# Forgetting attention: gate and mask in one tile that VectorE adds, and the second score products of two long query tiles on 64 rows each

## The chip, the cores and the metric

The kernel runs on one core of a Trainium2 chip. The metric is device time in microseconds (us), the median over runs of the same program. A core has TensorE (matrix products: a weight load brings a stationary operand of up to 128 rows and 128 columns into the array, a matmul then streams the columns of the moving operand through it), VectorE (DVE in the profile), ScalarE (ACT), GpSimd (POOL) and SyncE (SP), which mostly issues DMA transfers. Matmul results go to PSUM, which has banks of 512 float32 columns on 128 partitions; everything else on the chip lies in SBUF, also with 128 partitions.

## The reference

A decoder trunk of two layers on 512 tokens of width 1024. Each layer is a half-step SwiGLU feed-forward, a mixer of three parallel groups (short convolution, HGRN2 recurrence, forgetting attention called FoX), one output projection over all groups, and a second feed-forward. The change is in FoX, which has 8 heads of 64:

```python
log_f = jax.nn.log_sigmoid((f_logit + f_bias).astype(f32))
cum = jnp.cumsum(log_f, axis=1).transpose(0, 2, 1)
def block(i):                                   # 128 queries
    ...
    s = (jnp.einsum('bhqd,bhkd->bhqk', qb, kh).astype(f32)
         + (cb[..., :, None] - cum[..., None, :]))
    s = jnp.where(qpos[:, None] >= kpos[None, :], s, MASK_VALUE)
    p = jax.nn.softmax(s, axis=-1)
    return jnp.einsum('bhqk,bhkd->bhqd', p.astype(vh.dtype), vh)
```

The term of the query, `cb`, is the same for all keys of a row, so softmax doesn't see it; the kernel adds only minus the running sum of each key.

## The kernel before

All large products are made in a format with a rounded high part and a low part ("fp32r"): an operand x is split into hi (the rounded copy) and lo (x − hi), and a product is the sum of three, hi·hi, hi·lo and lo·hi. Weights are streamed from HBM, split by ScalarE (the cast to hi) and VectorE (the subtraction for lo), and multiplied by TensorE (lines 499, 505, 506 in `mm3`, 603 in `stream_steps`).

In each layer's mixer the steps of attention are woven with dense products (the remaining input projections, the convolution, the first three quarters of the output projection) by generators: `BESIDE` says how many pieces of dense work stand between two steps of `fox_attend`. Matmuls of the attention and of the pieces beside it are put in one written order by `follow("p", ...)`. The other engines' queues are ordered by the scheduler.

Heads are worked off in order. `fox_prep` (lines 1926 to 1950) makes the operands of one head two heads ahead: four transposes bring queries and keys of the head (64 rows each) to the partitions, ScalarE writes hi, VectorE lo, and six DMAs on SP's queue (line 1949) spread their halves over the tiles QA = [hi of q; lo of q], KA = [hi of k; hi of k], QB = [hi of q; two rows of ones] and KB = [lo of k; two rows of the sums]. QA·KA is hi·hi + lo·hi, on 128 rows; QB·KB is hi·lo plus the gate, on 66 rows. The two rows are minus the running sums, hi and lo, from `fox_decay`; they come from DRAM by a small DMA (line 1934), and GpSimd writes the ones (line 1935).

A head has two steps p, each with two query tiles u of 128 queries; query tile i = 2p + u sees n = 128(i + 1) keys. `scores(h, p)` makes for each query tile the product with QA and then the one with QB, into one PSUM area (line 1974 in the profile is the helper that records them): p = 0 has 128 and 256 columns in one bank, p = 1 has 384 and 512 in a bank each. There are two banks for it ("sc"), which the steps share in turn. Then `maximum` (line 1983) lets VectorE add the mask (zeros, and −1e30 above the diagonal in the last 128 columns) and take the row maximum in one pass, in place in PSUM; ScalarE takes the exponential (line 377), which frees the bank, and the weights are normalised (lines 2000 to 2006). Two steps later `turn` transposes the weights (line 2015), splits them (2030, 2031), and `values` multiplies them with V (line 2040).

The order within one round is: turn of step k, half of the values of the head before, preparation of head h + 2, scores of step k + 2, the other half of the values. HGRN2, earlier in the same stage, has products on tiles of 64 rows and 64 columns (line 1723 and others), of which four lie side by side on the array.

Of the kernel before, what the change touches and what calls it, by code (L numbers as in the profile page):

```python
# [8 lines left out]
F32 = mybir.dt.float32  # L9
# [5 lines left out]
ALU = mybir.AluOpType  # L15
# [201 lines left out]
def halves(x):  # L217

    return x.rearrange("p (h t) -> p h t", h=2)
# [17 lines left out]
def inner(x):  # L237

    return x.rearrange("p (b t h) -> p b h t", h=2, t=CH)
# [12 lines left out]
class Trunk:  # L252
# [40 lines left out]
    def build_consts(self, scratch):  # L293

        nc = self.nc
        c = self.const

        self.ones_blk = c.tile([P, P], F32R, tag="ones_blk", name="ones_blk")
        nc.vector.memset(self.ones_blk.bitcast(F32), 0.0)
        for h in range(2):  # L300
            r = slice(64 * h, 64 * h + 64)
            nc.vector.memset(self.ones_blk[r, r].bitcast(F32), 1.0 / 64)

        self.heads2 = c.tile([P, 2], F32, tag="heads2", name="heads2")
        nc.vector.memset(self.heads2, 0.0)
        for h in range(2):
            nc.vector.memset(self.heads2[64 * h : 64 * h + 64, h : h + 1], 1.0)

        self.smask = c.tile([P, T], F32, tag="smask", name="smask")
        nc.vector.memset(self.smask, 1.0)  # L310
        nc.vector.memset(self.smask.rearrange("p (c t) -> p c t", t=CH)[:, :, 0:1], 0.0)
        self.ones_row = nc.const_aps.tensor(1.0, [NH, T], F32)
        self.mask = c.tile([P, T], F32, tag="mask", name="mask")
        nc.vector.memset(self.mask[:, : 3 * P], 0.0)

        self.lmask = c.tile([P, 6, CH], U8, tag="lmask", name="lmask")
# [24 lines left out]
        b = scratch(F32)[:, :CH]  # L341
        for l in range(1, 7):
            nc.vector.tensor_scalar(
                a, xf, scalar1=float(2 ** (l - 1)), scalar2=None, op0=ALU.is_ge
            )
            nc.vector.tensor_scalar(b, xf, scalar1=float(2**l), scalar2=None, op0=ALU.is_lt)
            nc.vector.tensor_mul(a, a, b)
            nc.vector.tensor_mul(self.lmask[:, l - 1, :], a, own)

        nc.vector.tensor_scalar(  # L350
            inner(self.mask[:, 3 * P :])[:, 0], halves(later), scalar1=-1e30, scalar2=None, op0=ALU.mult
        )

    def n(self, s):
        self.uid += 1
# [996 lines left out]
    def mix(self, l, w, w_out, conv_w, out_gain, q_gain, k_gain, f_bias, next_gain, logits):  # L1352
# [3 lines left out]
        with tc.tile_pool(name=self.n("mix"), bufs=1) as mp:  # L1356
# [48 lines left out]
            with tc.tile_pool(name=self.n("hg"), bufs=1) as hp:  # L1405
                self.tt, self.tb = "t", 10

                b, kb, q, S = (pair(mp, tag) for tag in ("b", "kb", "q", "S"))
                negc = mp.tile([NH, 2, T], F32R, tag="n", name=self.n("negc"))
                bz = features([(H_F, 256)], ("mm", "mm"), lambda: self.end_norm(self.bank("pt"), hp))  # L1410
                if l == 0:
                    self.lower_bounds(logits, hp.tile([P, T], F32, tag="t", name=self.n("lb"), bufs=10))
# [416 lines left out]
    def fox_decay(self, mp, hp, zf, negc):  # L1829
# [9 lines left out]
        for j in range(4):  # L1839
            nc.tensor.transpose(cb[:NH, j * P : (j + 1) * P], lf[:, j, :], self.ident)  # L1840
        c = hp.tile([P, T], F32, tag="t", name=self.n("fc"), bufs=self.tb)[:NH, :]
        nc.vector.tensor_tensor_scan(c, self.ones_row, cb[:NH, :], 0.0, op0=ALU.mult, op1=ALU.add)
        nc.scalar.activation(negc[:, 0, :], c, AF.Copy, scale=-1.0)
        nc.vector.scalar_tensor_tensor(
            out=negc[:, 1, :], in0=c, scalar=-1.0, in1=negc[:, 0, :], op0=ALU.mult, op1=ALU.subtract
        )
        self.negc = self.dram.tile([NH, 2, T], F32, tag="negc", name=self.n("negc"))
        nc.sync.dma_start(self.negc, negc.bitcast(F32))

    def fox_qkv(self, mp, hp, tokens, half):  # L1850

# [67 lines left out]
    def fox_prep(self, pool, h, qk, g):  # L1919
# [6 lines left out]
        tl = lambda tag: self.mp.tile([P, T], F32R, tag=tag, name=self.n(tag))  # L1926
        hi, lo = tl("b0"), tl("b1")
        if h % 2:
            QA, KA, QB, KB = (tl(t) for t in ("S0", "S1", "q0", "q1"))
        else:  # L1930
            A = self.mp.tile([P, 2, T], F32R, tag="n", name=self.n("A"))
            QA, KA, QB, KB = A[:, 0, :], A[:, 1, :], tl("kb0"), tl("kb1")
        QB, KB = QB[:66, :], KB[:66, :]
        nc.sync.dma_start(KB[64:66, :].bitcast(F32), self.negc[h])
        nc.gpsimd.memset(QB[64:66, :].bitcast(F32), 1.0)
        b = self.bank("pt")
        for i in range(4):
            self.follow("p", nc.tensor.transpose(
# [3 lines left out]
        nc.vector.scalar_tensor_tensor(  # L1942
            out=lo, in0=b, scalar=g, in1=hi, op0=ALU.mult, op1=ALU.subtract
        )
        for to, src in (
            (QA[:64], hi[:64]), (KA[:64], hi[64:]), (KA[64:], hi[64:]), (QB[:64], hi[:64]),
            (QA[64:], lo[:64]), (KB[:64], lo[64:]),
        ):
            nc.sync.dma_start(to.bitcast(F32), src.bitcast(F32))
        return QA, QB, KA, KB  # L1950

    def fox_attend(self, pool, half, g):

# [8 lines left out]
            ops[h] = self.fox_prep(pool, h, half[h // 4], g)  # L1962

        def scores(h, p):
            QA, QB, KA, KB = ops[h]
            pb = pool.tile([P, (384, 896)[p]], F32, tag=f"P{p}", name=self.n("P"), bufs=2)
            s2 = lambda tag: pool.tile([P, 2], F32, tag=tag, name=self.n(tag), bufs=2)
            nm, rs = s2("nm"), s2("rs")
# [6 lines left out]
            for u in range(2):  # L1975
                i = 2 * p + u
                c, n = slice(i * P, (i + 1) * P), (i + 1) * P
                mm(at[u], QA[:, c], turned_in(KA[:, :n]), start=p == 1 or u == 0, stop=False)
                mm(at[u], QB[:, c], turned_in(KB[:, :n]), start=False, stop=True)
            to = [pb[:, :P], pb[:, P:]] if p == 0 else [pb[:, : 3 * P], pb[:, 3 * P :]]  # L1980

            def maximum(u):
                m = nc.vector.tensor_tensor_reduce(
                    at[u], at[u], self.mask[:, (3 - 2 * p - u) * P :], scale=-1.0, scalar=1e30,
                    op0=ALU.add, op1=ALU.min, accum_out=nm[:, u : u + 1],
                )
                self.maxima = m.ins.name
# [13 lines left out]
            for u in range(2):  # L2001
# [3 lines left out]
                else:  # L2005
                    nc.vector.tensor_scalar(to[u], to[u], scalar1=rs[:, o], scalar2=None, op0=ALU.mult)
            weights[h, p] = to

        def turn(h, p):

# [63 lines left out]
                nc.vector.tensor_sub(self.yl[kt], fo, self.yh[kt])  # L2074

        steps = [(h, p) for h in range(NH) for p in range(2)]
        prep(0)
        yield
        scores(0, 0)
# [155 lines left out]
```

## Time and profile before

| | |
|---|---|
| median of 3 runs | 1731.06 us (1731.04 to 1732.46) |
| the profiled execution's own time | 1730.99 us |
| its span in the profile | 1729.2 us |
| TensorE, matmuls: busy | 1724.9 us |
| VectorE busy | 1420.3 us |
| ScalarE busy | 1009.4 us |
| GpSimd busy | 176.2 us |
| attention stages (two layers) | about 434 to 530 us and 1290 to 1387 us |

In the rows of the profile L1974 is line 1974 of the kernel; PE is a matmul, PEld a weight load, which overlaps matmuls. Rows of the timeline give start, length, engine, line, operation, output and inputs, shapes, and in square brackets the idle time before it with what ended it. Matmuls are pipelined, so their lengths overlap: the distance from start to start tells what one costs. Rows of the groups give the count, the busy time in all, the mean in ns, and the idle time before them.

### The profile page before, as it was taken

To read this page: it belongs to the slowest core of one execution; us is meant where nothing else is said; L and a number is where in the kernel's file an instruction comes from. 1 tells how busy PE (TensorE), PEld (TensorE's weight loads), DVE (VectorE), ACT (ScalarE), POOL (GpSimd) and SP (SyncE) were. 2 spreads that over 40 slices of the span, in tenths; PEclk is the share of its full clock that TensorE was granted. 3 is DMA by queue.
4 is the path that set the end of the run, shared out by engine and by line. 5 is a ranking of instruction groups with operands and counts; after the bars stand their busy time and mean duration, and the time that the engine had idled before them with its cause. 6 is when DMAs were issued, how large, how long until landed. Compare 5 with 4: busy or idle time off the path is not lost.

```text
span 1729.2 us, 32556 instructions
## 1 busy us (share of the span) xinstructions
PE 1724.9 (100%) x13161; PEld 1623.3 (94%) x13161; DVE 1420.3 (82%) x1988; ACT 1009.4 (58%) x1406; POOL 176.2 (10%) x174
## 2 busy tenths in 40 slices
PE   9999999999999999999999999999999999999999
PEld 8999999888888999999989999998988889999998
DVE  7988787678888898888689887876888889788884
ACT  5565565465776565566446655555667765655651
POOL 0011120100000112012001111201000000120210
PEclk9999999999999999999999999999999999999999
DMA  7778784243543967878266787933435447678672
GB/s 218 185 149 194 185 178 111 72 128 87 151 129 98 241 149 157 206 163 171 86 193 168 178 180 178 191 87 80 116 96 146 127 126 203 159 150 228 144 161 97
DMA packets 249766, 262.28 MB, mean 152 GB/s; under 512 B 25816, under 2 KB 221152, under 8 KB 249616
## 3 DMA queue, kind: packets, MB, share of 16 engines
q1 hardware_dynamic: 197344, 192.02, 37.2%
q0 software_dynamic: 52256, 68.19, 24.4%
q8 instruction: 103, 1.69, 0.4%
q14 instruction: 47, 0.39, 0.1%
q10 hardware_dynamic: 16, 0.00, 0.0%
HBM read 226.15 MB, written 2.17 MB: 132 GB/s over the span
## 4 chain that ended last, share of the span: by engine, by line
PE 100%; DMA 0%; DVE 0%; issue 0%
PE mm L499 11%; PE mm L505 11%; PE mm L506 11%; PE mm L603 9%; PE pt L499 7%; PE pt L506 7%; PE pt L505 7%; PE sc L499 6%; PE sc L506 6%; PE sc L505 6%; PE po L505 3%; PE po L499 3%; PE po L506 3%; PE po L603 2%; PE sc L1974 1%; PE po L2040 1%
## 5 line engine op out<-in xcount | busy, mean ns | idle before, releaser
L1075 DVE TENSOR_TENSOR hl<-w,hl 128x1024 fp32r<-128x1024 f32 x279 | 341.4, 1224 | 97.6 <-ACT hl L1071 95.8
L1071 ACT CAST hl<-w 128x1024 fp32r<-128x1024 f32 x279 | 292.8, 1049 | 205.5 <-PE mm L506 50.3
L486 DVE TENSOR_TENSOR hl<-st,hl 128x1024 fp32r<-128x1024 f32 (+3 forms) x151 | 159.1, 1056 | 95.9 <-ACT hl L480 95.2
L480 ACT CAST hl<-st 128x1024 fp32r<-128x1024 f32 (+3 forms) x151 | 137.4, 913 | 155.5 <-PE po L506 37.0
L499 PE MATMUL mm<-xc,hl 128*128 128x256 f32 x698 | 191.5, 275 | 0.0
L505 PE MATMUL mm<-xc,hl 128*128 128x256 f32 x696 | 191.5, 275 | 0.0
L506 PE MATMUL mm<-xc,hl 128*128 128x256 f32 x696 | 191.4, 275 | 0.0
L499 PE MATMUL pt<-xc,hl 128*128 128x256 f32 x546 | 150.1, 275 | 0.0
L505 PE MATMUL pt<-xc,hl 128*128 128x256 f32 x544 | 149.7, 275 | 0.0
L506 PE MATMUL pt<-xc,hl 128*128 128x256 f32 x544 | 149.6, 275 | 0.0
L499 PEld LDWEIGHTS mm<-xc,hl 128*128 128x128 f32 x698 | 133.9, 192 | 0.1
L505 PEld LDWEIGHTS mm<-xc,hl 128*128 128x128 f32 x696 | 133.6, 192 | 0.0
L506 PEld LDWEIGHTS mm<-xc,hl 128*128 128x128 f32 x696 | 133.6, 192 | 0.0
L499 PE MATMUL sc<-xc,hl 128*128 128x256 f32 (+1 forms) x466 | 127.9, 275 | 0.0
L505 PE MATMUL sc<-xc,hl 128*128 128x256 f32 x464 | 127.7, 275 | 0.0
L506 PE MATMUL sc<-xc,hl 128*128 128x256 f32 x464 | 127.6, 275 | 0.0
L603 PE MATMUL mm<-hl,x 128*128 128x512 f32 x432 | 107.2, 383 | 0.0
L499 PEld LDWEIGHTS pt<-xc,hl 128*128 128x128 f32 x546 | 104.6, 192 | 0.3
L505 PEld LDWEIGHTS pt<-xc,hl 128*128 128x128 f32 x544 | 104.4, 192 | 0.3
L506 PEld LDWEIGHTS pt<-xc,hl 128*128 128x128 f32 x544 | 104.4, 192 | 0.0
L499 PE MATMUL mm<-x,hl 128*128 128x512 f32 x272 | 103.4, 381 | 0.0
L506 PE MATMUL mm<-x,hl 128*128 128x512 f32 x272 | 103.1, 379 | 0.0
(540 smaller groups left out, 5310.9 us busy)
## 6 DMA issues: line engine op xcount, KB each, us to landing
w<-in_ffn_w_in_dram SPq DMA_DIRECT2D x124, 512.0 KB, 6.0
w<-in_ffn_w_out_dram POOLq DMA_DIRECT2D x50, 512.0 KB, 9.5
w<-in_ffn_w_out_dram SPq DMA_DIRECT2D x49, 512.0 KB, 4.4
st<-in_ffn_w_out_dram SPq DMA_DIRECT2D x39, 512.0 KB, 3.6
st<-in_w_mix_in_dram SPq DMA_DIRECT2D x72, 256.0 KB, 3.1
st<-in_ffn_w_in_dram SPq DMA_DIRECT2D x71, 256.0 KB, 3.2
w<-in_ffn_w_in_dram POOLq DMA_DIRECT2D x29, 512.0 KB, 10.0
w<-S POOLq DMA_DIRECT2D x29, 512.0 KB, 5.1
```

Of the source, the lines that this page charges most:

```text
L480: a = nc.scalar.copy(hi, src[:, c : c + w])
L486: b = nc.vector.tensor_sub(lo, src[:, c : c + w], hi)
L499: i = nc.tensor.matmul(acc[:, c], ah, bh[:, c.start // 2 : c.stop // 2, :], start=first and c.start == 0, stop=False, skip_group_check=True,)
L505: nc.tensor.matmul(acc, ah, bl, start=False, stop=False, skip_group_check=True)
L506: i = nc.tensor.matmul(acc, al, bh, start=False, stop=last, skip_group_check=True)
L603: self.follow("p", self.nc.tensor.matmul(acc, *((w, woven(x)) if toks is None else (x[:, toks], woven(w))), start=k == 0 and id(acc) not i ...
L1071: A(nc.scalar.copy(hi, src))
L1075: return lambda: V(nc.vector.tensor_sub(lo, src, hi))
L1974: mm = lambda *a, **k: E(nc.tensor.matmul(*a, skip_group_check=True, **k))
L2040: E(nc.tensor.matmul(self.ob[:, o * P : (o + len(at)) * P], half[2][:, j, h].rearrange("p a d -> p (a d)"), turned_in(part[:, at[0] : at[- ...
```

## The change

The gate leaves TensorE. The sums are written once, in float32, to DRAM. `fox_gate(h, p)` broadcasts the first n of them to all 128 partitions, for each of the two query tiles, by a DMA on GpSimd's queue, and writes −1e30 above the diagonal in the last 128 columns by a select on GpSimd. VectorE's pass adds this tile where it added the mask. The gates of head h + 1 are asked for right after the scores of head h for the same p, and go into the same tiles.

The second product then has hi of q and lo of k alone: 64 rows. KB becomes [lo of k; lo of k]. For p = 0 both products are on 128 rows (QA·KB is hi·lo + lo·lo). For p = 1 the first of the two query tiles takes rows 0 to 63, the second rows 64 to 127; for that, QA holds the last 128 queries with its halves swapped. The two first products of a step are now issued ahead of the two second ones. `fox_prep` has eight DMAs, three of them for the swapped queries and the second copy of lo, and no longer the small one and the memset.

```diff
-        self.mask = c.tile([P, T], F32, tag="mask", name="mask")
-        nc.vector.memset(self.mask[:, : 3 * P], 0.0)
...
-        nc.vector.tensor_scalar(
-            inner(self.mask[:, 3 * P :])[:, 0], halves(later), scalar1=-1e30, scalar2=None, op0=ALU.mult
-        )
...
-        nc.scalar.activation(negc[:, 0, :], c, AF.Copy, scale=-1.0)
-        nc.vector.scalar_tensor_tensor(
-            out=negc[:, 1, :], in0=c, scalar=-1.0, in1=negc[:, 0, :], op0=ALU.mult, op1=ALU.subtract
-        )
-        self.negc = self.dram.tile([NH, 2, T], F32, tag="negc", name=self.n("negc"))
-        nc.sync.dma_start(self.negc, negc.bitcast(F32))
+        nc.scalar.activation(inner(negc), turned_out(c), AF.Copy, scale=-1.0)
+        self.negc = self.dram.tile([NH, T], F32, tag="negc", name=self.n("negc"))
+        nc.sync.dma_start(self.negc, negc)
...
-            QA, KA, QB, KB = (tl(t) for t in ("S0", "S1", "q0", "q1"))
+            QA, KA, KB = (tl(t) for t in ("S0", "S1", "q1"))
         else:
             A = self.mp.tile([P, 2, T], F32R, tag="n", name=self.n("A"))
-            QA, KA, QB, KB = A[:, 0, :], A[:, 1, :], tl("kb0"), tl("kb1")
-        QB, KB = QB[:66, :], KB[:66, :]
-        nc.sync.dma_start(KB[64:66, :].bitcast(F32), self.negc[h])
-        nc.gpsimd.memset(QB[64:66, :].bitcast(F32), 1.0)
+            QA, KA, KB = A[:, 0, :], A[:, 1, :], tl("kb1")
...
+        n, last = slice(0, 3 * P), slice(3 * P, T)
         for to, src in (
-            (QA[:64], hi[:64]), (KA[:64], hi[64:]), (KA[64:], hi[64:]), (QB[:64], hi[:64]),
-            (QA[64:], lo[:64]), (KB[:64], lo[64:]),
+            (QA[:64, n], hi[:64, n]), (KA[:64], hi[64:]), (KA[64:], hi[64:]), (QA[64:, n], lo[:64, n]),
+            (KB[:64, n], lo[64:, n]), (QA[64:, last], hi[:64, last]), (QA[:64, last], lo[:64, last]),
+            (KB[64:], lo[64:]),
         ):
             nc.sync.dma_start(to.bitcast(F32), src.bitcast(F32))
...
+    def fox_gate(self, h, p):
+        nc = self.nc
+        wide = lambda pool, tag: pool.tile([P, T], F32, tag=tag, name=self.n("W"))
+        if p == 0:
+            w = wide(self.mp, "kb0")
+            to = [w[:, :P], w[:, P : 3 * P]]
+        else:
+            to = [wide(self.mp, "q0")[:, : 3 * P], wide(self.const, "mask")]
+        for u, w in enumerate(to):
+            n = (2 * p + u + 1) * P
+            nc.gpsimd.dma_start(w, self.negc[h : h + 1, :n].to_broadcast([P, n]))
+        for w in to:
+            d = w[:, w.shape[-1] - P :].rearrange("p (t h) -> p t h", h=2)
+            nc.gpsimd.affine_select(
+                d, d, pattern=[[-1, CH], [-CH, 2]], compare_op=ALU.is_ge, fill=-1e30,
+                base=0, channel_multiplier=1,
+            )
+        self.gates[p] = to
...
                 mm(at[u], QA[:, c], turned_in(KA[:, :n]), start=p == 1 or u == 0, stop=False)
-                mm(at[u], QB[:, c], turned_in(KB[:, :n]), start=False, stop=True)
+            for u in range(2):
+                i = 2 * p + u
+                c, n = slice(i * P, (i + 1) * P), (i + 1) * P
+                r = slice(0, P) if p == 0 else (slice(0, 64), slice(64, P))[u]
+                mm(at[u], QA[r, c], turned_in(KB[r, :n]), start=False, stop=True)
...
-                    at[u], at[u], self.mask[:, (3 - 2 * p - u) * P :], scale=-1.0, scalar=1e30,
+                    at[u], at[u], gate[u], scale=-1.0, scalar=1e30,
...
             weights[h, p] = to
+            if h + 1 < NH:
+                self.fox_gate(h + 1, p)
...
+        self.gates = {}
+        for p in range(2):
+            self.fox_gate(0, p)
         prep(0)
```

More of the change, by code (lines that the diff above doesn't have):

```diff
@@ L1408, in mix @@
                 b, kb, q, S = (pair(mp, tag) for tag in ("b", "kb", "q", "S"))
-                negc = mp.tile([NH, 2, T], F32R, tag="n", name=self.n("negc"))
+                negc = mp.tile([NH, T], F32, tag="n", name=self.n("negc"))
                 bz = features([(H_F, 256)], ("mm", "mm"), lambda: self.end_norm(self.bank("pt"), hp))
@@ L1944, in fox_prep @@
         )
+        n, last = slice(0, 3 * P), slice(3 * P, T)
         for to, src in (
-            (QA[:64], hi[:64]), (KA[:64], hi[64:]), (KA[64:], hi[64:]), (QB[:64], hi[:64]),
-            (QA[64:], lo[:64]), (KB[:64], lo[64:]),
+            (QA[:64, n], hi[:64, n]), (KA[:64], hi[64:]), (KA[64:], hi[64:]), (QA[64:, n], lo[:64, n]),
+            (KB[:64, n], lo[64:, n]), (QA[64:, last], hi[:64, last]), (QA[:64, last], lo[:64, last]),
+            (KB[64:], lo[64:]),
         ):
             nc.sync.dma_start(to.bitcast(F32), src.bitcast(F32))
-        return QA, QB, KA, KB
+        return QA, KA, KB
+    def fox_gate(self, h, p):
[16 more added lines that the diff above has]
+        self.gates[p] = to
     def fox_attend(self, pool, half, g):
@@ L1964, in scores @@
         def scores(h, p):
-            QA, QB, KA, KB = ops[h]
+            QA, KA, KB = ops[h]
+            gate = self.gates[p]
             pb = pool.tile([P, (384, 896)[p]], F32, tag=f"P{p}", name=self.n("P"), bufs=2)
```

## The prediction

> **What bounds the kernel now.** I read the page first, the busy line and the chain that ended last.
>
> ```profile
> span 1729.2 us, 32556 instructions
> PE 1724.9 (100%) x13161; PEld 1623.3 (94%) x13161; DVE 1420.3 (82%) x1988; ACT 1009.4 (58%) x1406; POOL 176.2 (10%) x174
> PE 100%; DMA 0%; DVE 0%; issue 0%
> ```
>
> TensorE is busy from end to end and the chain never leaves it: what its own stream gains or loses, the kernel gains or loses, until another engine makes it wait. Second, the attention stage of the first layer (the second is alike) by windows, with columns for busy time and count of each engine:
>
> ```profile
> 434.00:530.00 96.00, 96.00 (x532) 85.76 (x530) 82.31 (x192) 69.24 (x152) 3.11 (x6) 1.00 0.51 133
> ```
>
> VectorE is busy for 82 of 96 us and GpSimd for 3: TensorE bounds here too, with full clock, VectorE not far behind. Third, the timeline of one score step of two long query tiles (head 4, layer 1 of 2), matmuls and then weight loads. A is the first product, on 128 rows; the one that reads kb is the second, on 66; I call them A0, B0, A1, B1.
>
> ```profile
> 493.32 0.41 PE L1974 MATMUL sc<-A 128*128 128x384 f32 x1
> 493.56 0.33 PE L1974 MATMUL sc<-kb,kb 66*128 66x384 f32 x1
> 493.73 0.38 PE L1974 MATMUL sc<-A 128*128 128x512 f32 x1
> 493.95 0.38 PE L1974 MATMUL sc<-kb,kb 66*128 66x512 f32 x1
> 494.17 0.38 PE L603 MATMUL mm<-hy,hl 128*128 128x512 f32 x1
> ...
> 493.29 0.19 PEld L1974 LDWEIGHTS sc<-A 128*128 128x128 f32 x1
> 493.40 0.19 PEld L1974 LDWEIGHTS sc<-kb,kb 66*128 66x128 f32 x1
> 493.57 0.19 PEld L1974 LDWEIGHTS sc<-A 128*128 128x128 f32 x1
> 493.73 0.19 PEld L1974 LDWEIGHTS sc<-kb,kb 66*128 66x128 f32 x1
> 493.95 0.41 PEld L603 LDWEIGHTS mm<-hy,hl 128*128 128x128 f32 x2
> ```
>
> Busy times overlap, so I go by starts. A matmul of 512 columns holds the array 0.22 us (493.73 to 493.95), one of 384 0.17 (493.56 to 493.73). The next weight load starts as the running matmul starts (493.73 and 493.95 stand in both lists), so it is hidden. A0's record is 0.08 longer than its likes: it began to stream at 493.40, 0.11 after its load, which is what a bare load costs. The step takes 494.17 − 493.40 = 0.77 us. There are 16: 8 heads, 2 layers.
>
> **The change, part by part.** *The halves.* B0 and B1 move to 64 rows each and stand side by side. If they run together, the shorter is hidden: −0.16 us a step. But TensorE goes from whole-array products to half-array ones and back. What does such a switch cost? The kernel has other products on parts of the array; the timeline at one of them, the way in and the way out:
>
> ```profile
> 400.72 0.59 PE L603 MATMUL po<-hl,x 128*128 128x512 f32 x2
> 401.24 0.19 PEld L1723 LDWEIGHTS pt<-t 64*64 64x64 f32 x5 [0.33 <-issue]
> ...
> 402.49 0.82 PE L1723 MATMUL pt<-t 64*64 64x32 f32 x44
> 403.24 0.48 PE L603 MATMUL mm<-hl,x 128*128 128x512 f32 x1
> ...
> 403.24 0.19 PEld L603 LDWEIGHTS mm<-hl,x 128*128 128x128 f32 x1
> ```
>
> In: the second L603 matmul starts at 400.72 + 0.59 − 0.38 = 400.93, and the next load not with it but at 401.24, 0.31 later; the profile knows no cause ("issue"). That is 0.07 before the matmul's recorded end. Out: the last small matmul starts at 402.49 + 0.82 − 0.22 = 403.09 (0.22 is the length of one of these records), and the load comes at 403.24, again 0.07 before the recorded end, though only 32 columns were to be streamed. So a load for another division of the array waits until the matmul ahead has run out. The new matmul then follows its load by 0.11, as above: L603's at 403.24 is recorded 0.10 longer than usual.
>
> These tiles divide rows and columns; ours only rows. One place divides rows alone, a transpose of 8 rows at the start:
>
> ```profile
> 2.45 1.06 PE L2157 MATMUL po<-const-bfloat16-1.0 128*128 128x512 bf16 x2
> 3.44 0.18 PEld L670 LDWEIGHTS pt<-ident,gr 8*128 8x128 f32 x1 [0.83 <-issue]
> ```
>
> The matmul ahead ends at 2.45 + 1.06 = 3.51, and the load starts at 3.44: the same 0.07, again without a known cause. I take the switch as priced at both ends. The Trainium skill ("TensorEngine Tiling (Array Packing)", Tiling Modes) says the same of every change of mode, that it drains the array; the two rows agree with it.
>
> Do the halves run together? The row of 402.49 has 44 matmuls with starts (0.82 − 0.22) / 43 = 0.014 us apart, each with its own load of 64 columns, which alone would take half of 0.11: four tiles load and run at once. I give the second half 0.01.
>
> The new order is A0, A1, B0, B1. From A0's stream: A1 after 0.16; B0 after a further 0.31 + 0.11; B1 0.01 later; the next whole-array product after 0.31 + 0.11. Sum 1.01 against 0.77: +0.24 us a step, 16 × 0.24 = **+3.8 us**. Bounds of this price: without any switch cost −0.15 a step, −2.4 us; with both switches and the halves one after the other 0.24 + 0.16, +6.4 us. I take the value between, which the nearest rows give.
>
> *A1's earlier turn.* Its bank must be free, which ScalarE's exponentials of the step before decide. At head 2:
>
> ```profile
> 469.82 0.20 ACT L377 ACTIVATION_READ_ACCUMULATOR P<-sc,nm 128x1 f32 x1
> 470.07 0.19 PEld L1974 LDWEIGHTS sc<-A 128*128 128x128 f32 x1
> ```
>
> The load of A1 waited there until 470.07, just behind the read that ended at 470.02. Now it is wanted 0.16 earlier, so this wait grows by up to 0.16, once a layer: 0 to 0.3 us, since TensorE comes 0.24 later at each of the steps ahead; I take 0.2.
>
> *The short step* (128 and 256 columns): 66 rows become 128, all in whole-array form; four loads of 0.11 set its pace in either order. Nothing.
>
> *VectorE, ScalarE.* The pass that takes the maxima reads the gate tile instead of the mask, in the same shapes. The first mask and the low part of the sums fall away off the path. Nothing; if VectorE had to wait at it, the bank of the row above would be late next.
>
> *SP's queue.* Per head eight copies for six, and two rows less: at 0.64 a place, the last copy is issued 1.3 later. At head 2:
>
> ```profile
> 458.38 1.75 SPq L1949 DMA_DIRECT2D A<-b  x3
> 461.47 0.59 SPq L1949 DMA_DIRECT2D kb<-b  x1
> ...
> DMA to landing us min/median/max: 2.2/2.3/3.4
> ...
> 465.62 0.19 PEld L1974 LDWEIGHTS sc<-A 128*128 128x128 f32 x1
> ```
>
> The last lands at 461.47 + 1.28 + 2.3 = 465.05, and the third load of the step, now B0's, stands at 465.62: covered, by 0.6. With the slowest landing, 3.4, it is 0.5 late, once a layer: 0 to 1.1 us; I take 0. The weights of the output projection queue behind these copies and come 1 us later; their buffers are refilled well before use.
>
> *The gates on GpSimd.* Per step two broadcasts of the sums to 128 partitions (64 to 256 KB) and two selects, in place of a memset; each pair waits until VectorE has read the pair of the head before. The trace has no such copy; its nearest rows:
>
> ```profile
> L1371 POOL DMA_DIRECT2D fb<-in_fox_f_bias_dram x2 | 1.2, 592 | 0.0
> masks.py:199 POOL TENSOR_SCALAR_AFFINE_SELECT ident<-ident 128x128 f32<-128x128 f32 x1 | 0.3, 284 | 0.0
> ...
> fb<-in_fox_f_bias_dram POOLq DMA_DIRECT2D x2, 4.0 KB, 3.1
> w<-S POOLq DMA_DIRECT2D x29, 512.0 KB, 5.1
> ...
> 457.78 0.29 DVE L1983 CUSTOM_DVE_ANT_0 sc<-sc,mask 128x128 f32<-128x128 f32 x1
> 521.68 0.29 DVE L1983 CUSTOM_DVE_ANT_0 sc<-sc,mask 128x128 f32<-128x128 f32 x1
> ```
>
> A gate costs its second issue's start (0.6), the landing (3.1 to 5.1) and a select or two (0.3 to 0.6): 4.0 to 6.3 us, GpSimd waiting the while; two a head, 8.0 to 12.6. A head lasts (521.68 − 457.78) / 6 = 10.7. In proportion to size the landings come to 3.6 and 4.1, the head to 0.6 + 3.6 + 0.3 and 0.6 + 4.1 + 0.3, some 9.5: covered by 1.2 us. I take 0.
>
> **Sum**, against this execution's own 1730.99 us (its span of 1729.2 and 1.8 around it): + 3.8 + 0.2 = 1735.0; the median of the runs shown is 0.07 higher, which changes nothing.
>
> **The rivals.**
>
> *No switch cost.* If rows alone can be divided without running the array out, the hidden B0 is all that is left: 1731.0 − 2.4 = 1728.6, not slower. For it: the 66-row products of today come and go without any gap (493.56, 493.73). Against it: the 8-row load, and the tiles with 64 rows. The Trainium skill ("TensorE: Matmul & The Clock Gate", Part 3, the span model) counts such a pack as one matmul and 4 ns for each further tile, without a term for coming and going; by it, this rival would be the result.
>
> *Only one of the switches costs,* in or out: 0.24 − 0.20 = 0.04 a step, 1731.6.
>
> *The halves do not run together:* the change would not do what it says. B1 waits for B0: +6.4, 1737.4. Against it the 0.014.
>
> *The gates come late.* Once two gates take more than a head's 10.7 us, every maximum waits for GpSimd, then the exponentials, the bank, and TensorE. At the upper price it is 1.9 us for each of six heads in two layers, 1754; where only the tightest steps are caught, a few us, 1737 to 1742.
>
> **How the numbers follow.** Forecast (both switches, halves together) 0.62, its own range 1734.2 to 1736.0; no switch cost 0.13; one switch 0.07; halves in sequence 0.08; late gates 0.10. The range 1731.3 to 1739.0 leaves out the second, and of the last the dearer half. A difference below 0.2%, 3.5 us, can't be told from none here, so the forecast itself lies just above that: I count four fifths of it as slower (0.50), with the last two cases 0.68. Same: 0.12 of the forecast, most of the cheap cases, 0.28. Faster by over 3.5 us isn't reached even without switch costs: 0.04.
>
> **What would show it.** In the new timeline, after A1 starts: B0's load 0.31 later and not at once; B0 and B1 within 0.02; the next whole-array load 0.31 after B1. A short gap at B0's load alone means one switch. A second select that ends after VectorE's maximum was due, and idle time there put down to GpSimd, means late gates; a wait of B0's load in the short step, late copies. The forecast is wrong if loads of B0 follow A1 at once, or if TensorE's busy share falls.

## The result, and the profile after

| | before | changed |
|---|---|---|
| median of 5 runs | 1731.14 us (1731.04 to 1732.46) | 1746.93 us (1745.75 to 1748.46) |
| ratio | | 1.009, 95% interval 1.0076 to 1.0105 |
| the profiled execution's own time, its span | 1730.99, 1729.2 us | 1745.75, 1743.6 us |

The kernel became slower, as forecast, but by 15.8 us and not by 4: the time lies 8 us above the range. The mean granted clock of TensorE was 1.000 in the run of 1745.75, 0.998 in that of 1748.46 and 0.999 in the other three of the changed kernel; 0.001 of the span is 1.7 us, so the 1.2 us between the median and the profiled execution, the run of 1745.75, are about what the clock takes.

The page of the changed kernel: span, the busy line, and the chain that ended last.

```profile
span 1743.6 us, 32786 instructions
PE 1730.5 (99%) x13161; PEld 1619.7 (93%) x13161; DVE 1423.0 (82%) x1984; ACT 1009.2 (58%) x1406; POOL 255.1 (15%) x286
PE 20%; DMA 1%; POOL 0%; SPq 0%; DVE 0%; issue 0%
```

TensorE is busy for 5.6 us more, but the span is 14.4 us longer, so most of the loss is TensorE standing still. GpSimd is 79 us busier. The chain, which never left TensorE before, now does; the view follows it back over a fifth of the span, to 1357.85, and its earliest part, in order of time, lies in the second layer's attention:

```profile
1357.85 0.55 POOL W L1953
1358.40 5.77 DMA W<-negc
1364.22 0.66 POOL W L1956
1364.88 0.55 POOL W L1953
1365.43 4.93 DMA W<-negc
...
1377.63 4.12 DMA W<-negc
1381.81 0.72 POOL W L1956
1382.63 0.43 DVE sc L1998
...
1386.17 5.27 DMA q<-b
1391.49 0.49 PE sc L1985 x2
```

Issue, broadcast, select, issue, broadcast, select, four gates in a row with no engine but GpSimd; then VectorE's maximum, which waited for the last of them, the operand copies behind it, one of which takes 5.27 us to land, and from there on the chain is almost wholly TensorE's. Both causes that the experiments below find are in these lines.

The attention stage of the first layer by windows, with the columns of the view in the prediction (the stage is now longer, so the window is too):

```profile
434.00:545.00 111.00, 107.29 (x577) 91.82 (x576) 88.95 (x199) 76.12 (x161) 35.45 (x56) 1.00 0.67 159
```

TensorE stands idle for 3.7 of 111 us where it was busy for all of 96, GpSimd has gone from 3 to 35 us, and the DMA share from 0.51 to 0.67. If the ends of the 13161 matmuls are compared one by one, in order, the two kernels part in the two attention stages, by 6.3 us in the first and by 8.2 in the second; elsewhere they stay within 0.4 us of each other.

**The long step** of head 4, layer 1, by the timeline, first the matmuls, then the weight loads:

```profile
496.53 0.93 PE L2032 MATMUL pt<-ident,P 128*128 128x128 f32 x7
497.22 0.62 PE L1985 MATMUL sc<-A 128*128 128x384 f32 x2
497.77 0.48 PE L1985 MATMUL sc<-kb,A 64*128 64x384 f32 x2
498.19 0.70 PE L597 MATMUL mm<-hy,hl 128*128 128x512 f32 x2
...
497.77 0.19 PEld L1985 LDWEIGHTS sc<-kb,A 64*128 64x128 f32 x2 [0.28 <-issue]
498.18 0.73 PEld L597 LDWEIGHTS mm<-hy,hl 128*128 128x128 f32 x4 [0.23 <-issue]
```

A1 starts at 497.22 + 0.62 − 0.38 = 497.46; the load of the first half comes 0.31 later, with no cause that the profile knows. Both halves are inside one stretch of 0.48, the length of the longer alone with its bare load, so they run together. The load of the next whole-array product comes 0.41 after theirs. The second product behind the step starts at 498.19 + 0.70 − 0.38 = 498.51, 1.29 after A0's record; before it was 494.39 − 493.32 = 1.07. A step costs 0.22 more, 16 steps 3.5 us.

**The wait that fills the rest.** The timeline of head 3, short step (p = 0): GpSimd, VectorE, TensorE.

```profile
473.35 0.70 POOL L1956 TENSOR_SCALAR_AFFINE_SELECT W<-W 128x128 f32<-128x128 f32 x1 [2.58 <-DMA W<-negc]
474.99 0.71 POOL L1956 TENSOR_SCALAR_AFFINE_SELECT W<-W 128x128 f32<-128x128 f32 x1 [0.94 <-DMA W<-negc]
475.64 1.09 POOL L1953 DMA_DIRECT2D W<-negc  x2
479.73 1.41 POOL L1956 TENSOR_SCALAR_AFFINE_SELECT W<-W 128x128 f32<-128x128 f32 x2 [3.00 <-DMA W<-negc]
481.08 1.09 POOL L1953 DMA_DIRECT2D W<-negc  x2
...
480.46 0.30 DVE L1998 CUSTOM_DVE_ANT_0 sc<-sc,W 128x128 f32<-128x128 f32 x1 [2.21 <-POOL W L1956]
...
481.51 0.75 DVE L1930 SCALAR_TENSOR_TENSOR b<-pt,qkg,b 128x512 fp32r<-128x512 f32 x1
...
482.41 0.52 PE L2032 MATMUL pt<-ident,P 128*128 128x128 f32 x3 [2.02 <-DVE b L1930]
```

Read it from the end. TensorE waits 2.02 us for a bank that VectorE frees with the low part of the next operands (L1930). That instruction needs nothing from GpSimd; it stands behind the maximum of the short step, which waits 2.21 us for the select of its gate. And GpSimd is not late by accident: it issues two broadcasts (475.64), waits 3.00 us for them, selects twice, and only then issues the next two (481.08). There is no idle time in it but the waits for its own transfers. GpSimd's groups in the first layer's window (count, busy us, mean ns, idle us before them), the select's row over the whole run, and the whole run's waits:

```profile
L1956 POOL TENSOR_SCALAR_AFFINE_SELECT W<-W 128x128 f32<-128x128 f32 x28 | 20.8, 745 | 47.8 <-DMA W<-negc 47.6
L1953 POOL DMA_DIRECT2D W<-negc x28 | 15.3, 546 | 34.2 <-DVE nm L1998 34.2
...
L1956 POOL TENSOR_SCALAR_AFFINE_SELECT W<-W x64: 699/706/3649, 397.7 to 1399.4; 128x128 f32<-128x128 f32 x64
...
PE pt L2032 <- DVE b L1930: 4.7, 2, 2.7
PE sc L1985 <- DMA q<-b: 2.6, 3, 1.1
...
DVE sc L1998 <- POOL W L1956: 16.0, 21, 2.2
```

(The select's durations: least, middle, greatest, in ns; waits: total us, times, longest.) Fourteen gates take 20.8 us of selects, 47.8 of waiting for the broadcasts and 15.3 of issues: 83.9 us, 6.0 a gate, 12.0 a head. The 34.2 lie ahead of the first of them. A head had 10.7 before. VectorE waits for selects 21 times, 16.0 us in all.

**The copies** of the operands, SP's queue (line 1939 there), time from issue to landing (least, middle, greatest):

```profile
DMA to landing us min/median/max: 1.9/3.9/6.6
```

They took 2.2/2.3/3.4 before. That is the second row of the waits above: TensorE waits 2.6 us for them.

### The profile page after: what moved, and what is told of

It is laid out like the page before. It is cut to its first block, busy times and chain, and to the rows that moved or that the text cites. A ratio compares the mean times of both kernels' runs of the same rounds, so it can differ in the third digit from the quotient of the medians.

```text
span 1743.6 us, 32786 instructions
## 1 busy us (share of the span) xinstructions
PE 1730.5 (99%) x13161; PEld 1619.7 (93%) x13161; DVE 1423.0 (82%) x1984; ACT 1009.2 (58%) x1406; POOL 255.1 (15%) x286
```

## The experiments

**A** is the theory that the gates come late: GpSimd's chain of landing and selects is longer than a head, and this is what lies beyond the forecast. The rival to it is that the array switches, or the copies on SP's queue, cost more than I had counted. **C** is that the broadcasts hold up the operand copies. **D** came last, from a trace of the runs: a select on GpSimd and an instruction of VectorE hold each other up. Times are medians; ratios, with their 95% interval, are against the kernel before (1731.1 us). The diffs are against the changed kernel, unless the text names another.

### The first head's gates for all heads

```diff
-            if h + 1 < NH:
-                self.fox_gate(h + 1, p)
```

No gate is made after the first head's; the sums of the other heads are left out.

> The gates of head 0 serve all eight heads (the sums of the other heads are left out): no broadcast and no select runs during the attention; halves, swapped queries and eight copies a head stay. In the trace of the changed kernel each long step costs 0.22 us more than before, 16 times, 3.5 us; the other 11 to 12 us are stalls. Theory A, the gates are late (one takes GpSimd some 5.9 us, two a head, and VectorE's queue waits behind its maximum): the stalls go, 1734.6. Theory B, the operand copies are late because SP's queue has eight instead of six: up to 3.6 us stay, 1735.5 to 1738.2. Theory C, the broadcasts slow the copies on the DMA engines: as A, 1734.6. Under 1733 the price of the switch would be wrong.

Measured: 1735.62 us (1735.02 to 1737.13), ratio 1.0027 (1.0016 to 1.0037). Of the 15.8 us, 11.3 go with the later gates. What is left, 4.5, is close to the 4.0 that I had forecast without them. The copies' landing is back:

```profile
DMA to landing us min/median/max: 1.8/2.2/3.6
```

By the ends of the matmuls against those of before, the two attention stages together take 4.3 us more: 3.5 for the 16 steps, and 0.8 at head 2, of which 0.27 a layer is the wait at A1.

### Whole rows for the second products

```diff
-                r = slice(0, P) if p == 0 else (slice(0, 64), slice(64, P))[u]
+                r = slice(0, P)
...
```

The second products are on 128 rows everywhere, so nothing changes the array's division, and `fox_prep` has six copies again; the gates stay as in the changed kernel. Then the same with the first head's gates for all heads.

> The second products of the long step on all 128 rows, six copies a head, nothing swapped; the gates stay as in the changed kernel. No switch of the array. A: 3.5 us less than the changed kernel, 1743.4, or less than that saved (1743.4 to 1746), because TensorE, quicker by 0.22 a step, runs into gates that are as late as before. B: the stalls at the copies go too, 1739.8. C: as A.

> Both together: gates of head 0 for all heads (the others' sums left out) and whole rows with six copies. All theories: 1731.1, the time before, within 0.5. More would show a cost that none of them has; less, that the two rows of the gate or the memset cost something before.

Measured: 1748.29 us (1747.20 to 1748.43), ratio 1.0096 (1.0082 to 1.011), with the gates; 1732.04 (1731.72 to 1733.21), ratio 1.0004 (0.9995 to 1.0013), without the later ones. So the switches are worth 3.6 us (1735.62 − 1732.04) when the gates are in time, as 16 × 0.22 says, and nothing when they are late. (The clock doesn't hide a gain: the profiled execution of the first took 1748.27 us with one stretch of 3.4 us at half clock, so about 1746.6 without, still above the 1745.75 of the changed kernel at full clock.) That missed what I expected of the first of the two, which was some gain. VectorE's wait tells why:

```profile
DVE sc L1997 <- POOL W L1955: 23.0, 28, 2.2
```

It went from 16.0 to 23.0 us. TensorE came to each step earlier and waited there: GpSimd set the pace. The second missed too, by a little: 0.9 above the time before, where I expected no more than 0.5. By the ends of the matmuls that 0.9 is in the attention, 0.4 and 0.5 us in the two layers, all of it at the scores of head 2; its cause wasn't followed.

### The halves one after the other

```diff
-                r = slice(0, P) if p == 0 else (slice(0, 64), slice(64, P))[u]
+                r = slice(0, P) if p == 0 else slice(0, 64)
...
```

Both second products of a long step on rows 0 to 63, six copies, the first head's gates for all heads.

> First gates (the sums of the other heads left out), six copies, and both second products of the long step on rows 0 to 63, one after the other: the same two switches, but no pairing. If the halves run together in the changed kernel, this costs 0.16 more a step than the run with first gates alone, 2.6 us, less what two copies fewer save (up to 0.8): 1737.4 to 1738.2. If they did not run together, 1735.6 or less.

Measured: 1737.17 us (1737.02 to 1738.55), ratio 1.0037 (1.0024 to 1.005), 1.55 above the kernel with upper and lower half (which has eight copies a head) and 0.2 under the range I gave. The step of head 4, layer 1:

```profile
495.39 0.64 PE L1984 MATMUL sc<-kb,A 64*128 64x384 f32 x2
495.96 0.92 PE L597 MATMUL mm<-hy,hl 128*128 128x512 f32 x3
```

From the halves to the next product it is 0.57 here and was 0.42: a pair on upper and lower half gains 0.15, the shorter product, so the halves do run together. Sixteen times 0.15 are 2.4, of which 0.9 doesn't reach the end. By the ends of the matmuls this kernel's attention stages are 6.0 us longer than before, which is 16 × 0.37 and nothing more: the 0.8 at head 2 of the kernel with upper and lower half is gone. Whether the slower step or the six copies did that isn't shown. The gain is far under what the two switches take, 0.22 + 0.15 = 0.37 a step.

### The broadcasts ahead of the selects

```diff
-        for w in to:
-            ...affine_select(...)
-        self.gates[p] = to
+        self.loaded.append((p, to))
+        if len(self.loaded) > 1:
+            self.fox_mask()          # the selects of the gate before, then self.gates[p] = to
```

The aim: GpSimd issues a gate's broadcasts before it selects in the gate before, so that it never waits for the transfer that it has just issued. The first kernel has these lines alone; the second also writes the order of GpSimd's instructions out, with `follow("g", ...)` around both.

> The result is complete. The two broadcasts of a gate are issued as in the changed kernel, but its selects only after the broadcasts of the next gate: GpSimd no longer waits for a landing, and has 2 x (1.1 + 1.4) = 5.0 us of work a head. Same bytes, same number of everything. A: the gates come in time, 1734.6. C: the copies still land late, 1734.6 to 1738.2, with PE waits put down to the copies (0.3 at head 2, 1.3 at head 5 in the changed kernel) and none to GpSimd. If what counts were the work of GpSimd and not its waiting for a landing, 1743 or more.

> As the run with the broadcasts ahead of the selects, but with GpSimd's order written out: there GpSimd still ran two broadcasts, two selects, two broadcasts, one gate after the other from 452.7 us on, as in the changed kernel, so it tested nothing. Theory A now reads: GpSimd is one unbroken chain of gates, 14 a layer of 5.95 us each (1.1 for two issues, the landing, 0.7 for a select, or two), 83 us, and that chain sets the pace; the switches lie beneath it, which is why whole rows saved nothing. With the landing out of the chain GpSimd has 5 us of work a head and A gives the 1735.6 of the run with first gates alone. C, copies that land late because the broadcasts share the DMA engines: up to 3.6 on top, 1735.6 to 1739.2. If the work of GpSimd or the bytes set the pace: 1745 or more.

The first, 1748.04 us (1746.24 to 1749.41), ratio 1.0096 (1.0082 to 1.0109), tested nothing: the scheduler put the selects back right behind their own broadcasts. The second: 1738.35 us (1738.25 to 1739.11), ratio 1.0043 (1.0029 to 1.0056). With the same transfers, the same selects and the same result as the changed kernel, the order on GpSimd alone is worth 8.6 us by the medians, and 7.4 between the two profiled executions, both at a clock of 1.000. The waits of its TensorE and VectorE:

```profile
PE sc L1991 <- DMA kb<-b: 1.1, 2, 0.6
PE sc L1991 <- DMA q<-b: 0.9, 2, 0.6
...
DVE sc L2004 <- POOL W L1962: 1.8, 4, 0.7
```

VectorE's 16.0 us are down to 1.8. TensorE's waits for operand copies are still there, and the time is 2.7 us above the kernel without later gates.

### Both: broadcasts ahead, whole rows

> Complete result: whole rows with six copies, and GpSimd's order written out with the broadcasts ahead. No switch, no chain. A: 1732.0, as with first gates and whole rows. C: up to 3.6 more. In any case 3.5 under the same with halves if TensorE sets the pace in both.

Measured: 1735.74 us (1735.27 to 1736.79), ratio 1.0027 (1.0016 to 1.0038). It is 2.6 below the kernel with halves, not the 3.5 that I expected "in any case", and 3.7 above A's 1732.0, just beyond the 3.6 that I gave C. The gate on VectorE, without any halves and with the better order, is still slower than the kernel before.

### A cheaper select

```diff
-            d = w[:, w.shape[-1] - P :].rearrange("p (t h) -> p t h", h=2)
+            d = w[:, w.shape[-1] - P :]
-                d, d, pattern=[[-1, CH], [-CH, 2]], ...
+                d, d, pattern=[[-1, P]], ...
```

The select runs over 128 columns in a row, not over the same 128 adjacent columns as a pattern of 64 × 2; it masks the wrong columns.

> The changed kernel with selects over 128 columns in a row instead of two interleaved halves (so the wrong columns are masked; same count, same elements, same waits). If the stride makes a select 0.71 us where the one in a row at the start of the program takes 0.28, a gate gets 0.43 to 0.85 shorter, 5.1 to 5.5 us, 14 of them 71 to 77 us, which end at 523 to 528 us, before the 529 of the last maximum in the kernel before: A gives 1735.6 to 1740. If the select is 0.7 either way, or the chain of gates is not what sets the pace: 1746 to 1748.

Measured: 1742.71 us (1740.71 to 1745.10), ratio 1.0068 (1.0055 to 1.0081). The select and TensorE's wait, then windows around that wait with the granted clock in the third column from the end:

```profile
L1956 POOL TENSOR_SCALAR_AFFINE_SELECT W<-W x64: 287/292/3062, 398.0 to 1395.2; 128x128 f32<-128x128 f32 x64
...
PE sc L1985 <- DMA kb<-b: 4.0, 2, 2.0
```

```profile
466.40:468.40 2.00, 0.03 (x1) 0.00 (x0) 1.88 (x4) 2.00 (x6) 0.44 (x1) 1.00 0.78 180
...
468.90:472.00 3.10, 3.10 (x11) 2.65 (x10) 2.46 (x10) 1.50 (x5) 1.22 (x3) 0.50 0.83 208
```

The select is 0.29 us instead of 0.71, and VectorE waits for GpSimd once, 0.4 us. But the time is not where A put it, 1735.6 to 1740. The copy that B0 of head 2 needs came 2.0 us late in each layer; behind that the granted clock was 0.50 for some 3.4 us, which takes another 1.7. Two layers of 3.7 us are 7.4 of the 11.6 lost. (The one run of five at a clock of 1.000 took 1740.71.) As a test of A this run is weak: TensorE's own stalls gave GpSimd time. I read it so that the gates moved and the broadcasts fell on other copies; that how late a copy comes hangs on which transfers it meets is not shown by itself.

### Narrow broadcasts

Two kernels in which, from the second head on, each broadcast brings 64 KB (the last 128 columns) instead of 64 to 256; the other columns keep the first head's sums. One has the broadcasts ahead, the other GpSimd's order of the changed kernel.

```diff
+        if h:
+            to = self.wide[p]            # from the second head on the first head's tiles
...
+            c = slice(n - P if h else 0, n)
-            nc.gpsimd.dma_start(w, self.negc[h : h + 1, :n].to_broadcast([P, n]))
+            nc.gpsimd.dma_start(w[:, c], self.negc[h : h + 1, c].to_broadcast(...))
```

> The kernel whose GpSimd sends a gate's broadcasts ahead of the selects of the gate before (1738.35), but from the second head on each broadcast brings only the last 128 columns of its tile, 64 KB instead of 64 to 256 KB; the other columns keep the first head's sums, so those are left out of the later heads. As many transfers, waits and selects, 0.4 of the bytes. In the run with whole broadcasts TensorE still waits for operand copies (2.0 us in 4 waits), whose landing has gone from 2.3 to 3 to 5 us. Theory C (the broadcasts' bytes hold up the copies): copies land in 2.2 to 2.8 us, these waits fall below 0.5 us, 1735.3 to 1736.6 us, the time of the kernel that keeps the first head's gates (1735.62). Rival: the copies are late because there are more transfers, whatever their size, or because they are issued late: landing stays at 3 to 5 us, 1737.5 to 1738.6.

> The changed kernel, with GpSimd's own order (two broadcasts, two selects, then the next gate), but from the second head on each broadcast brings only the last 128 columns, 64 KB; the first head's sums stay in the others. Theory A (the chain of landing and two selects is longer than half a head, and the landing is a latency that bytes change little: 4.0 us at 64 KB, 4.7 at 256): a gate takes 0.55 + 4.0 + 0.7 to 5.9, two of them 10.9 to 11.6 against 10.7 a head, VectorE still waits for GpSimd's selects; 1737 to 1743 us, at least 1 us above the run with the broadcasts ahead and narrow. Rival (the landing is long only through its bytes): a gate falls to some 4.5 us, no waits of VectorE, 1735.3 to 1736.6.

Measured: 1738.26 us (1737.33 to 1738.49), ratio 1.004 (1.0027 to 1.0052), with the broadcasts ahead; 1738.16 (1737.45 to 1739.78), ratio 1.0041 (1.0027 to 1.0055), in the old order. Both missed. In the first the waits for copies are gone, as C said, though the copies still land in 3.0 us (median); but the time didn't go. The second's time lies in the range that I gave A, by luck: it is not 1 us above the first, and VectorE hardly waits. A gate is short enough there:

```profile
476.30 1.09 POOL L1957 DMA_DIRECT2D W<-negc  x2
479.50 1.36 POOL L1960 TENSOR_SCALAR_AFFINE_SELECT W<-W 128x128 f32<-128x128 f32 x2 [2.11 <-DMA W<-negc]
480.82 1.08 POOL L1957 DMA_DIRECT2D W<-negc  x2
```

From issue to issue 4.52 us, where the changed kernel had 5.44 at the same place: GpSimd waits 2.1 and not 3.0 for its data. Two gates take 9.0 us of a head's 10.7, and the chain no longer delays anyone (VectorE waits 0.3 us once); what TensorE still waits for are copies, 1.5 us in two waits. I had taken the landing for a latency; it depends on the bytes, and not on the transfer's own alone: a broadcast of 64 KB lands in 3.3 us here (median) and in 4.0 in the changed kernel, beside larger ones. So the chain comes from both, bytes and selects.

Why was the first not faster? Its timeline, at head 2, with a short step's scaling of the weights by the reciprocal (L2031 there, L2021 in the changed kernel); the second fence is the changed kernel's scaling, one head on:

```profile
471.52 1.37 POOL L1966 TENSOR_SCALAR_AFFINE_SELECT W<-W 128x128 f32<-128x128 f32 x2
...
471.87 1.25 DVE L2031 TENSOR_SCALAR P<-P,rs 128x128 f32<-128x128 f32 x2
```

```profile
482.84 0.55 DVE L2021 TENSOR_SCALAR P<-P,rs 128x128 f32<-128x128 f32 x2
```

Beside a select, the two scalings take 1.25 us and not 0.55. That gave theory D. In the changed kernel's order they are not stretched (means of 348 and 296 ns for 256 and 128 columns, 347 and 287 before).

### Broadcasts ahead, without selects

```diff
-        for w in to:
+        for w in to if h == 0 else ():
```

The two kernels with the broadcasts ahead, narrow and whole, without the selects from the second head on; those heads are not masked.

> The kernel with narrow broadcasts sent ahead (1738.26), without GpSimd's selects from the second head on: these heads are not masked, and only the last 128 columns of their sums are brought. Theory D (a select and VectorE's scaling of the weights by the reciprocal hold each other up: with the selects ahead the scaling of 256 columns takes 742 ns and not 348, that of 128 columns 853 and not 287): both fall back to 348 and 287 ns, and the time to 1735.3 to 1736.6 us, that of the kernel that keeps the first head's gates (1735.62). Rival (what is left of the loss comes from the transfers): the scaling falls back all the same, but the time stays at 1737.3 to 1738.5.

> The kernel with whole broadcasts sent ahead (1738.35), without GpSimd's selects from the second head on: these heads are not masked. Theory C (the broadcasts' bytes hold up the operand copies): TensorE still waits for copies, 1 to 2 us in 4 or so waits, at least 0.5 us above the run with narrow broadcasts and no selects: 1736.2 to 1737.8. If the selects alone cost what is left, 1735.3 to 1736.2; if the transfers alone do, 1738 to 1738.6.

Measured: 1735.30 us (1734.68 to 1737.29), ratio 1.0026 (1.0016 to 1.0035), narrow; 1737.13 (1736.38 to 1737.34), ratio 1.0034 (1.0021 to 1.0046), whole. The scaling in the narrow kernel, at the first head's step, where a select still runs, and at head 2, the place of the fence above:

```profile
452.48 1.25 DVE L2031 TENSOR_SCALAR P<-P,rs 128x128 f32<-128x128 f32 x2
470.89 0.55 DVE L2031 TENSOR_SCALAR P<-P,rs 128x128 f32<-128x128 f32 x2
```

D holds in what it says of the scaling: where the selects go, the long scaling goes too (the means stay above 348 and 287 ns only by the first head), and the narrow kernel is as fast as the one without later gates. That the scaling is all that the selects cost isn't shown: with them VectorE also waits 1.8 us in all, four times, for a select, in both kernels with the broadcasts ahead, and without them never. C holds too: whole broadcasts cost 1.8 us more than narrow ones by the medians, with no select in either; the copies land in 4.0 us and not in 2.9, and TensorE waits for copies in the whole one alone (0.8 us, twice).

How much each is worth is read better from the traces than from the medians: us by which the two attention stages together are longer than before, by the ends of the matmuls, in the four kernels with the broadcasts ahead.

| | without later selects | with them |
|---|---|---|
| narrow broadcasts | 4.3 | 6.5 |
| whole broadcasts | 4.9 | 7.2 |

The bytes cost 0.5 to 0.7 us and the selects 2.2 to 2.3, either way. The rest of what the medians differ by lies outside the attention: of the 1.3 us between the two profiled executions without selects, 0.3 ahead of the first attention and 0.4 behind the last matmul.

## Why the prediction was wrong

The steps of medians lead from the kernel before to the changed one:

| | us | step |
|---|---|---|
| before | 1731.1 | |
| halves, with gates of the first head alone | 1735.6 | +4.5 |
| narrow broadcasts ahead, no selects | 1735.3 | −0.3 |
| whole broadcasts | 1737.1 | +1.8 |
| selects | 1738.35 | +1.2 |
| each select behind its own broadcast | 1746.9 | +8.6 |

(The split of the +1.8 and the +1.2 is not to be trusted: in the attention itself it is 0.5 and 2.3, by the table above. The last step, 7.4 between executions at full clock, is the chain of gates, which the prediction put at nothing: in the profiled execution the changed kernel's attention stages are 14.5 us longer than before, 7.3 more than with the broadcasts ahead.)

*The halves*: right. I had 0.31 + 0.11 in, 0.01 between the halves, 0.31 + 0.11 out, +0.24 a step and +3.8 in all; measured 0.31 in, no distance between the halves, 0.41 from their loads to the next load, +0.22 a step, 3.5 us, and 3.6 by taking the switches out. The Trainium skill's rule that a change of the array's mode drains it ("TensorEngine Tiling (Array Packing)", Key Properties) agrees with the trace; the span model without such a term ("TensorE: Matmul & The Clock Gate", Part 3) would have had the step faster.

*A1's earlier turn*: 0.2 taken for two layers, 0.3 at most; without late gates it was 0.27 a layer, 0.5 in all.

*The short step* and *VectorE, ScalarE*: the first cost nothing, as taken, but for head 2, where the kernels with the first head's gates alone lose 0.2 to 0.3 us in each layer's short step. Of the second, "if VectorE had to wait at it, the bank of the row above would be late next" is what happened; the bank was another, the one that L1930 frees, behind the same maximum.

*SP's queue*: "I take 0" failed. The cover of 0.6 us was worked out with a landing of 2.3, a number of a trace that had no broadcasts; beside them the landing was 3.9. I had even priced the slowest, 0.5 a layer, 1.1 in all, and without the chain that bound held: in the kernel without later selects TensorE waits 0.8 us for the copies, and the bytes cost 0.5 to 0.7. In the changed kernel, with the chain, the wait is 2.6 us.

*The gates on GpSimd*: this is the step that failed. "some 9.5: covered by 1.2 us. I take 0." A head's two gates took 12.0 us, 1.3 more than the head. The landings in the changed kernel, over the whole run (KB, median us from issue):

```profile
W<-negc POOLq DMA_DIRECT2D x16, 256.0 KB, 4.8
...
W<-negc POOLq DMA_DIRECT2D x16, 128.0 KB, 4.4
```

The sum had 4.1 and 3.6 for these two, in proportion to size between rows of other transfers; that is 1.5 us a head. It had 0.3 for a select, which took 0.71, 0.9 more a head: the row that it came from walks 128 columns in a row, this one the same number as a pattern of 64 × 2, and in a row it took 0.29 here too. With these, 0.55 + 4.4 + 0.71 and 0.55 + 4.8 + 0.71 are 11.7; the last 0.3 I put down to both selects often following the landing (at 479.73 above), where the sum counted one. The rival "the gates come late" then gave the right mechanism and condition, "once two gates take more than a head's 10.7 us", and the time fell between its two prices, 1737 to 1742 and 1754. I gave it 0.10, and left its dearer half out of the range. With a cover of 1.2 us out of 10.7, and two of three terms taken from rows of another shape, that was too little.

*The signs* that I named came: the select that ends behind the maximum's turn with idle time put down to GpSimd, and TensorE's busy share falling, from 100% to 99%.

What stays open: how the 2.2 us of the selects, with the broadcasts ahead, divide between the stretched scalings and VectorE's waits for the selects; no run parts the two. And the 0.8 to 0.9 us at head 2 that stay without later gates, of which A1's wait is a part.

## What to carry to other kernels

When work moves to an engine that was idle, price it as a loop: what it waits for itself, every instruction at its own shape, against the time of one round; where the sum comes close to the round (here 9.5 of 10.7), take the late case as the likely one, because it is paid on every round and not once. Write the order so that an engine never waits for the transfer that it has just issued; here that was 8.6 us at the same work, 7.4 of it at full clock. And two halves of the array gain at most the shorter product, here 0.15 us, against 0.37 for the two switches: pair them only where several such products share one switch.

## What the runs showed that I had not expected

- **A scaling on VectorE waits out the selects on GpSimd.** The rows above: 0.55 us for two scalings alone, 1.25 beside the selects, at the same place with and without them. The two selects end at 471.52 + 1.37 = 472.89; the first scaling began at 471.87 between them and lasted 1.12 us, to 472.99, where it takes 0.29 alone. The Trainium skill says that GpSimd and VectorE share one pair of ports of SBUF as an exclusive lock, held for a whole instruction ("SBUF — State Buffer", SBUF: two separate sides); the trace agrees.
- **A stall of 2.0 us can halve TensorE's clock for 3.4 us, or not, by where it falls.** It did so in both layers of the kernel with the cheaper select (the windows above), and not behind the wait of 2.02 us of the changed kernel's profiled execution, whose window from 480 to 483 us has a clock of 1.00:

```profile
480.00:483.00 3.00, 0.98 (x9) 0.73 (x7) 1.78 (x7) 1.28 (x5) 2.17 (x4) 1.00 0.67 156
```

  In every trace here, the stretches at one clock are whole multiples of 3.413 us, but for the last, which the end of the record cuts. If each trace is cut at these steps, TensorE was busy for 1.02 to 1.56 of 3.41 us in the five pieces (in three traces) that a piece at 0.50 follows, and for 1.71 to 2.43 in the eight others (in two traces) that are less than three quarters busy; behind those the clock stayed full. The wait of the changed kernel was shared by two pieces, from 478.01 and from 481.43, with 2.38 and 2.43 us busy.

  The Trainium skill has a free-running window of 3413 ns and two clocks, half and full ("TensorE: Matmul & The Clock Gate", Part 1); the 0.50 agrees, but by its text the clock falls after an idle window of about 3.4 us, and here less was enough.
- **A select over a pattern of 64 × 2 costs more than twice one over 128 columns in a row**: 706 against 292 ns for 128x128, on the same adjacent columns. What in the pattern costs it isn't shown.
- **A MB of GpSimd's broadcasts takes more of the DMA engines than a MB of the other transfers.** By queue (packets, MB, share of the 16 engines) in the first layer's window of the changed kernel:

```profile
q1 hardware_dynamic: 12906, 12.89, 43.2%
q0 software_dynamic: 1568, 4.59, 23.4%
```

A MB of the broadcasts takes 5.1% of the window, one of the other transfers 3.4%.
